# Expert weights of a mixture-of-experts stage as 2 MB tiles of 16 KB rows instead of 512 KB tiles of 4 KB rows

## The chip, the cores and the metric

The kernel runs on one core of one Trainium2 chip. The metric is the device time of one execution in microseconds; a version's time is the median of its runs. All data are float32. MB is a million bytes, but a tile called 512 KB or 2 MB holds 524,288 or 2,097,152 bytes.

## The reference, cut to what matters

The block has a mixing part (two gated branches over 512 rows of 1024 columns, called the front part here) and an expert part, which is what the change is about:

```
h = rmsnorm(x, g_ffn)                                  # 512 x 1024
aff = softmax(h @ w_router)                            # 16 experts
vals, idx = top_k(aff.T, 64)                           # every expert takes 64 rows
xe = h[idx]                                            # 16 x 64 x 1024
gt = einsum('ecd,edf->ecf', xe, w_gate)                # 16 x 64 x 2048
up = einsum('ecd,edf->ecf', xe, w_up)
ye = einsum('ecf,efd->ecd', silu(gt) * up, w_down) * vals
x  = x + scatter_add(ye, idx);  out = rmsnorm(x, g_final)
```

Each of the 16 experts has three matrices of 1024 x 2048 floats (w_down 2048 x 1024), 8.39 MB each: 48 matrices, 402.65 MB, each used once.

## The kernel before, in words

The front part projects with weights that are split in two fp32r halves. `w_raw` loads a raw column block into a `wr` tile (four buffers), `w_prep` splits it into `wh` (ScalarE) and `wl` (GpSimd), two buffers each, and `proj` multiplies. At the end `wo_load` and `wo_prep` do the same for `w_o` (its halves lie in `hT2`, a single tile that holds 16 slices), and a loop of 16 jobs (line 1076) multiplies by it and makes the router's logits (`turn`, `logits`).

Experts are served in pairs `pr` (expert 2pr in output rows 0 to 63, expert 2pr+1 in rows 64 to 127). A pair's 2048 hidden columns are done in two halves `c`. For each half `gate_part`, `up_part` and `down_part` go through eight weight tiles per expert; a tile is 128 x 1024 floats, 4 KB in one piece per partition. `unit_mm` holds the matmuls of gate and up. `gather` picks the pair's rows by matmuls with a one-hot matrix (line 1182) once per pair, `scatter` adds the pair's results to `xm` (line 1275). `down_part` of a half runs behind `gate_part` of the next.

All expert tiles are loaded by SyncE's queue at line 1010. The list `wq` has them in the order of use, and `WS` names for each the buffer it goes to: 38 buffers of 512 KB that are used in turn (`hA`, `we0`, `wh`, `wl`, `wr`, `we1`, `we2`), and seven more (`sg`, `st`, `ye`, `hh`) that serve once before their other use begins. Buffers belong to pools that open when the front part's pools close: `hA` and `we0` after the last projection, `we1` and the pool `T` (`sg`, `hh` and others) after the router's logits, `we2` after the top-64 search. `e_load(n)` issues the next n loads: 28, then 14, then 3, then 8 after every fourth weight tile of each expert. SyncE waits in order: a load whose buffer is still read holds up all loads behind it.

Of the kernel before, what the change touches and what calls it, by code (L numbers as in the profile page):

```python
# [25 lines left out]
EPS = 1e-6  # L26
KT = D // 128
# [3 lines left out]
for _n, _w in (("g_mix", 8), ("ca_w", 32), ("ca_b", 8), ("b_r", 16), ("b_i", 16), ("lam", 16),  # L31
               ("cb_w", 72), ("cb_b", 24), ("fbias", 16), ("g_ffn", 8)):
    CV[_n] = (_o, _w)
    _o += _w
# [7 lines left out]
    "W": ("right", dict(wr=4, wh=2, wl=2)),  # L42
# [10 lines left out]
    "hA": ("left", dict(hA=8)),  # L53
    "G": ("left", dict(tga=5)),
# [4 lines left out]
    "we0": ("left", dict(we0=12)),  # L59
    "T": ("right", dict(hh=4, xe=1, pm=1, sel=1, sg=1, st=1, ye=1)),  # L60
    "rout": ("right", dict(work=1, msk=1, aff=1, mx=1, sm=1, m8=1)),
    "we1": ("left", dict(we1=7)),
    "we2": ("left", dict(we2=3)),
# [34 lines left out]
def block_kernel(ctx, tc, A, out, dbg=None):  # L98
# [102 lines left out]
    for nm, c0 in (("w_in", 5120), ("w_a_out", 0)):  # L201
        wlist += [(nm, c0 + i * 128) for i in range(8)]
    wraw, wsp = {}, {}
# [759 lines left out]
    def wo_load(q):  # L963
        rs_ = []
        for j in range(2):
            r = t_([128, KT, 128], nm="wr")
# [15 lines left out]

    wq = []
    for v in range(17):
        order = [("w_gate", v), ("w_down", v - 1), ("w_up", v)]
        if v == 15:
            order[:2] = order[1::-1]
        for nm, n in order:
            if 0 <= n < 16:
                for u in range(8):  # L990
                    for e in (n // 2 * 2, n // 2 * 2 + 1):
                        wq.append((nm, e, n % 2, u))
    wq.insert(35, wq.pop(15))
    wtile = {}
    wn = [0]
    WS = ("hA",) * 8 + ("we0",) * 12 + ("wh", "wl") * 2 + ("wr",) * 4 + ("we1",) * 7 + ("we2",) * 3
    WS0 = WS[:35] + ("sg", "st", "ye") + ("hh",) * 4 + WS[35:]

    def e_load(n):
        for i in range(wn[0], min(wn[0] + n, len(wq))):  # L1000
            nm, e, c, u = wq[i]
            tag = WS0[i] if i < len(WS0) else WS[(i - len(WS0)) % len(WS)]
            t = t_([128, 1024], nm=tag)
# [7 lines left out]
            wtile[nm, e, c, u] = t  # L1011
            if i == len(wq) - 1:
                for hf in range(2):
                    for t_i, s_i in (last2, (t, src)):
                        h = slice(hf * 512, (hf + 1) * 512)
                        SY.dma_start(out=t_i[:, h], in_=s_i[:, h])
            last2 = t, src
        wn[0] = min(wn[0] + n, len(wq))

    def w_of(nm, e, c):  # L1020
        return [wtile.pop((nm, e, c, u)) for u in range(8)]

    for i in range(8):
# [3 lines left out]
        if i in (4, 5):  # L1027
            wo_load(i - 4)
# [3 lines left out]
    close_("G", "mB")  # L1032
    open_("pers", "we0", "xo")
    xm = t_([128, 4, D], nm="xm")
    for i in range(4):
# [11 lines left out]
    e_load(28 - wn[0])  # L1047
# [28 lines left out]
    for u, (q, i) in enumerate(jobs):  # L1076
# [12 lines left out]
        if i == 3 and q < 2:  # L1089
            wo_prep(q + 2)  # L1090
        if q == 2 and i == 3:
# [17 lines left out]
    e_load(14)  # L1109
# [43 lines left out]
    e_load(3)  # L1153
# [8 lines left out]

    def gather(pr, nb=2):

        pm = t_([128, 4, 128], nm="pm")
        for i in range(4):
            for e in range(2):
                o = pm[:, i, e * 64:(e + 1) * 64]
                pos = pT[:, i, 2 * pr + e:2 * pr + e + 1]
                if hh:  # L1170
# [3 lines left out]
        xe = t_([128, KT, 128], nm="xe")  # L1174
        yield xe
        n = KT // nb
        for b in range(nb):
            p = p2("m", 2)
            for k in range(n):
                c = (b * n + k) * 128  # L1180
# [3 lines left out]
            tt(V, xe[:, b * n:(b + 1) * n, :], p[:, 0:n * 128].rearrange("p (k c) -> p k c", k=n),  # L1184
               win(cv, [[1, n], [0, 128]], CV["g_ffn"][0] + b * n), ALU.mult)
# [22 lines left out]
    def unit_mm(out, xe, wa, wb, ks=range(KT)):  # L1208

        for k in ks:  # L1210
            for hf in range(2):
                for o, w in ((0, wa), (64, wb)):
                    T.matmul(out[hf][o:o + 64], lhsT=xe[:, k, o:o + 64], rhs=w[k][:, hf * 512:(hf + 1) * 512],  # L1213
                             start=(k == 0), stop=(k == KT - 1))
            if k in (3, 7):
                e_load(8)

    sg = []

    def gate_part(pr, c, xe):  # L1220
        ea, eb = 2 * pr, 2 * pr + 1
        pg = [p2("gu", 3), p2("gu", 3)]
        wa, wb = w_of("w_gate", ea, c), w_of("w_gate", eb, c)
        if pr == 0 and c == 0:
            next(first)
            for k in range(0, KT, 2):
                next(first)
                next(first, None)
                unit_mm(pg, xe, wa, wb, (k, k + 1))
        else:  # L1230
            unit_mm(pg, xe, wa, wb)
        if not sg:
            sg.extend((t_([128, 2, 512], nm="sg"), t_([128, 2, 4, 128], nm="st")))
        return pg

    def silu(pg):
        for hf in range(2):
            act(sg[0][:, hf, :], pg[hf], AF.Silu)

    def up_part(pr, c, xe):  # L1240
        ea, eb = 2 * pr, 2 * pr + 1
        pu = [p2("gu", 3), p2("gu", 3)]
        unit_mm(pu, xe, w_of("w_up", ea, c), w_of("w_up", eb, c))
        for hf in range(2):
            tt(V, sg[0][:, hf, :], sg[0][:, hf, :], pu[hf], ALU.mult)

    def down_part(pr, c, acc, between=lambda j: None):
        ea, eb = 2 * pr, 2 * pr + 1
        wa, wb = w_of("w_down", ea, c), w_of("w_down", eb, c)

        def turned(g):
            p = p2("tr", 1)
            for j in range(4):
                T.transpose(p[:, j * 128:(j + 1) * 128], sg[0][:, g, j * 128:(j + 1) * 128], ident)  # L1254
            act(sg[1][:, g].rearrange("p j c -> p (j c)"), p)
# [3 lines left out]
        for j in range(8):  # L1259
            for hf in range(2):  # L1260
                for o, w in ((0, wa), (64, wb)):
                    T.matmul(acc[hf][o:o + 64], lhsT=sg[1][:, j // 4, j % 4, o:o + 64],  # L1262
                             rhs=w[j][:, hf * 512:(hf + 1) * 512],
                             start=(c == 0 and j == 0), stop=(c == 1 and j == 7))
            if j == 0:
                turned(1)
            between(j + 1)
            if j in (3, 7):
                e_load(8)

    def scatter(ye, sc):
        for i in range(4):
            for hf in range(2):
# [4 lines left out]
                tt(V, v, v, p, ALU.add)  # L1278

    def ye_of(acc):  # L1280
        ye = t_([128, D], nm="ye")
        for hf in range(2):
            act(ye[:, hf * 512:(hf + 1) * 512], acc[hf])
        return ye
# [3 lines left out]
    last = []  # L1288

    def last_smat():  # L1290
        gfin = t_([128, D], nm="we0")
        SY.dma_start(out=gfin, in_=A["g_fin_b"])
# [4 lines left out]
        a = t_([128, D], nm="ye")[:, 0:S]  # L1297
# [5 lines left out]
        last.extend((oh, gfin))  # L1303

    hh = []

    def norms():

        for i in range(4):
            hh.append(t_([128, D], nm="hh"))  # L1310
            act(hh[i], xm[:, i, :], AF.Copy, scale=rs2[:, i:i + 1])
# [8 lines left out]
    later = {0: lambda: rows(1, 1, "gu", 3)}  # L1320
    first = gather(0, 8)
    xe = next(first)
    pend = None
    prev = None
    for pr in range(8):
        acc = [p2("acc", 2), p2("acc", 2)]
        for c in range(2):
            end = pr == 7 and c == 1
            if end:
                down_part(*prev)  # L1330
                prev = None
                last_smat()
            pg = gate_part(pr, c, xe)
            if pr == 0 and c == 1:
                norms()
            if prev is not None:
                down_part(*prev)
                if prev[1] == 1:
                    pend = (ye_of(prev[2]), smat(pr - 1))
            silu(pg)  # L1340
            if end:
                rows(0, 0, "m", 2)
                rows(0, 1, "m", 2)
                rows(1, 0, "gu", 3)
            if c == 1 and pr < 7:
                *_, nxe = gather(pr + 1)
            up_part(pr, c, xe)
            prev = (pr, c, acc)
            if c == 0 and pend:
                scatter(*pend)  # L1350
                pend = None
        xe = nxe

    preload(AF.Sqrt)
    oh, gfin = last
    down_part(*prev, lambda j: later.pop(j, lambda: None)())
    rows(2, 0, "gu", 3)
    yh = t_([128, D], F32R, nm="ye")
# [6 lines left out]
    hh = [t_([128, D], nm="hh") for _ in range(4)]  # L1365

# [154 lines left out]
```

## Time and profile before

| what | before |
|---|---|
| median of 3 runs (lowest to highest) | 1668.33 us (1667.86 to 1669.81) |
| the profiled execution: its own time / its span | 1668.91 us / 1667.1 us |
| TensorE (PE) busy | 1576.9 us, 95% of the span |
| VectorE / ScalarE / GpSimd busy | 593.4 / 370.3 / 375.1 us |
| packets of SyncE's and the other hardware queue q1 | 220272, 487.11 MB, 77.7% of 16 engines' span |

The span runs from the first to the last instruction; 1.8 us of the execution's own time lie around it. TensorE's busy time has modelled ends of matmuls in it, so 95% does not say that TensorE is what bounds the kernel: the chain of waits and the stretches by time do. The share of the DMA engines is the mean over 16 engines, and can exceed 100% because the packets of one engine overlap a little.

### The profile page before, as it was taken

How to read it: one execution, taken by the hardware profiler on the slowest of the kernel's cores; microseconds unless marked ns; L12 is line 12 of the kernel's file. 1: busy time of each engine (PE TensorE's matmuls, PEld its weight loads, DVE VectorE, ACT ScalarE, POOL GpSimd, SP SyncE). 2: the span in 40 equal slices, each digit the busy share in tenths (PEclk: the TensorE clock that was granted, in tenths of full speed). 3: DMA queues.
4: the chain of work that ended last, by engine and by line, in shares of the span. 5: the costliest groups of instructions: out<-in, count | busy, mean ns of one | idle time of the engine just before them, and what ended most of it. 6: DMA issues, size and time to landing. Idle time of an engine off the chain costs nothing.

```text
span 1667.1 us, 19022 instructions
## 1 busy us (share of the span) xinstructions
PE 1576.9 (95%) x7348; PEld 892.0 (54%) x7348; DVE 593.4 (36%) x872; ACT 370.3 (22%) x581; POOL 375.1 (23%) x256
## 2 busy tenths in 40 slices
PE   8999899999999999899999999999999999999996
PEld 5788788878888889534334343243242242242232
DVE  7887878786665663510010100200200200200103
ACT  5443322347565433201000000000000000000002
POOL 3646565557555741000000000000000000000000
PEclk9999999999999999999999999999999999999999
DMA  6566342543333329899999999999999999999996
GB/s 202 171 200 208 123 115 83 151 139 95 97 106 89 88 88 314 322 384 407 408 408 409 409 408 409 409 409 409 409 408 409 409 409 409 409 408 408 406 409 245
DMA packets 223046, 491.87 MB, mean 295 GB/s; under 512 B 17803, under 2 KB 112331, under 8 KB 222956
## 3 DMA queue, kind: packets, MB, share of 16 engines
q1 hardware_dynamic: 220272, 487.11, 77.7%
q10 hardware_dynamic: 2236, 1.98, 0.4%
q0 software_dynamic: 448, 1.57, 0.3%
q8 instruction: 58, 0.95, 0.2%
q14 instruction: 32, 0.26, 0.0%
HBM read 473.82 MB, written 16.78 MB: 294 GB/s over the span
## 4 chain that ended last, share of the span: by engine, by line
DMA 34%; PE 29%; DVE 2%; ACT 1%; issue 0%; SPq 0%; DVEq 0%; ACTq 0%
PE q L1213 11%; DMA we<-in_w_down_dram 7%; DMA we<-in_w_gate_dram 6%; DMA we<-in_w_up_dram 5%; PE q L1262 4%; PE q L1182 4%; PE ps L239 3%; PE ps L1084 3%; PE q L1275 3%; DMA hA<-in_w_up_dram 3%; DMA wr<-in_w_down_dram 2%; DMA hA<-in_w_down_dram 2%; DMA wh<-in_w_down_dram 2%; DMA hA<-in_w_gate_dram 2%; DMA wh<-in_w_up_dram 2%; DMA wr<-in_w_gate_dram 1%
## 5 line engine op out<-in xcount | busy, mean ns | idle before, releaser
L1213 PE MATMUL q<-we,xe 128*64 128x512 f32 x1160 | 322.5, 599 | 11.8 <-DMA we<-in_w_gate_dram 4.3
L128 POOL TENSOR_TENSOR hh<-hh,we 128x512 f32<-128x512 f32 x2 | 3.0, 1483 | 953.8 <-ACT hh L125 953.8
L128 POOL TENSOR_TENSOR wl<-wr,wh 128x1024 fp32r<-128x1024 f32 x72 | 181.1, 2519 | 145.1 <-ACT wh L125 66.1
L239 PE MATMUL ps<-hT,wh 128*128 128x512 f32 x880 | 210.4, 391 | 0.0
L1213 PEld LDWEIGHTS q<-we,xe 128*64 128x64 f32 x1160 | 97.0, 136 | 206.8 <-issue 138.5
L1262 PE MATMUL q<-we,st 128*64 128x512 f32 x600 | 177.5, 603 | 13.1 <-ACT st L125 6.7
L239 PEld LDWEIGHTS ps<-hT,wh 128*128 128x128 f32 x880 | 164.6, 188 | 35.3 <-issue 0.8
L125 ACT ACTIVATE st<-q 128x512 f32<-128x512 f32 x32 | 19.1, 597 | 701.8 <-PE q L1254 701.8
L128 DVE TENSOR_TENSOR xe<-q,cv 128x512 f32<-128x512 f32 (+1 forms) x22 | 11.4, 543 | 379.0 <-PE q L1213 362.7
L1213 PE MATMUL q<-hA,xe 128*64 128x512 f32 x472 | 136.5, 600 | 4.8 <-DMA hA<-in_w_up_dram 2.3
L239 PE MATMUL ps<-hT,wl 128*128 128x512 f32 x440 | 110.2, 393 | 0.6 <-POOL wl L128 0.6
L1262 PEld LDWEIGHTS q<-we,st 128*64 128x64 f32 x600 | 51.1, 136 | 108.7 <-issue 57.3
L131 DVE SCALAR_TENSOR_TENSOR pm<-q,slotc,pm 128x512 f32<-128x512 f32 x7 | 5.3, 751 | 255.7 <-ACT pm L125 255.7
L125 ACT ACTIVATE wh<-wr 128x1024 fp32r<-128x1024 f32 x72 | 76.2, 1058 | 90.4 <-PE ps L239 46.8
L239 PEld LDWEIGHTS ps<-hT,wl 128*128 128x128 f32 x440 | 83.6, 190 | 18.6 <-POOL wl L128 1.1
L1213 PEld LDWEIGHTS q<-hA,xe 128*64 128x64 f32 x472 | 41.3, 136 | 76.8 <-issue 50.7
L128 DVE TENSOR_TENSOR sg<-sg,q 128x512 f32<-128x512 f32 x32 | 21.3, 684 | 168.1 <-PE q L1213 168.1
L1213 PE MATMUL q<-wr,xe 128*64 128x512 f32 x188 | 65.3, 600 | 1.4 <-DMA wr<-in_w_up_dram 1.2
L239 PE MATMUL ps<-hA,wh 128*128 128x512 f32 x256 | 61.4, 392 | 0.0
L1262 PE MATMUL q<-hA,st 128*64 128x512 f32 x172 | 55.1, 603 | 3.4 <-ACT st L125 2.2
L1275 PE MATMUL q<-ye,pm 128*128 128x512 f32 x112 | 53.9, 619 | 0.0
L239 PEld LDWEIGHTS ps<-hA,wh 128*128 128x128 f32 x256 | 48.1, 188 | 10.5
(321 smaller groups left out, 2274.6 us busy)
## 6 DMA issues: line engine op xcount, KB each, us to landing
we<-in_w_down_dram SPq DMA_DIRECT2D x149, 512.0 KB, 10.2
we<-in_w_up_dram SPq DMA_DIRECT2D x147, 512.0 KB, 10.2
we<-in_w_gate_dram SPq DMA_DIRECT2D x143, 512.0 KB, 10.2
hA<-in_w_gate_dram SPq DMA_DIRECT2D x67, 512.0 KB, 10.2
wr<-in_w_in_dram SPq DMA_DIRECT2D x56, 512.0 KB, 4.3
hA<-in_w_up_dram SPq DMA_DIRECT2D x51, 512.0 KB, 10.2
hA<-in_w_down_dram SPq DMA_DIRECT2D x42, 512.0 KB, 10.2
wr<-in_w_down_dram SPq DMA_DIRECT2D x33, 512.0 KB, 10.2
```

Of the source, the lines that this page charges most:

```text
L125: P.activation(out=out, in_=in_, func=func, **kw)
L128: e.tensor_tensor(out=out, in0=a, in1=b, op=op)
L131: V.scalar_tensor_tensor(out=out, in0=a, scalar=s, in1=b, op0=op0, op1=op1)
L239: T.matmul(p, lhsT=a[:, k, :], rhs=b[k], start=(n == 0), stop=(n == 23))
L1084: T.matmul(p, lhsT=a[k][:, i * 128:(i + 1) * 128], rhs=wo[q][b][:, k, :], start=(n == 0), stop=(n == 23))
L1182: T.matmul(p[:, k * 128:(k + 1) * 128], lhsT=hh[i][:, c:c + 128] if hh else xm[:, i, c:c + 128], rhs=pm[:, i, :], start=(i == 0), stop=(i ...
L1213: T.matmul(out[hf][o:o + 64], lhsT=xe[:, k, o:o + 64], rhs=w[k][:, hf * 512:(hf + 1) * 512], start=(k == 0), stop=(k == KT - 1))
L1262: T.matmul(acc[hf][o:o + 64], lhsT=sg[1][:, j // 4, j % 4, o:o + 64], rhs=w[j][:, hf * 512:(hf + 1) * 512], start=(c == 0 and j == 0), sto ...
L1275: T.matmul(p, lhsT=sc[:, i * 128:(i + 1) * 128], rhs=ye[:, hf * 512:(hf + 1) * 512], start=True, stop=True)
```

## The change

An expert weight tile becomes 2 MB. For gate and up it is 256 rows of the full 2048 columns, two neighbouring rows per partition (row = 256u + 2p + r); for down it is 512 rows of 1024 columns, four neighbouring rows per partition. Either way 16 KB lie in one piece per partition in memory. `gather` takes every second column of its source (and a reordered `g_ffn`, `GX`), and the transposes of `down_part` every fourth, so that the operands fit these rows. A unit is now a whole pair: gate, up and down each go through four pairs of tiles over all 2048 columns, with four PSUM buffers for gate and up.

Buffers are slots of 16 KB per partition: two in `hz` (the place of `hA`), three in `we0`, one each in `whl`, `wring`, `we1`, `we2`, and one each in `sgy` and `hh` that serves once first. `wring` and `whl` are single tiles that take the place of the `wr`, `wh` and `wl` tiles. `e_load` issues as many loads as there are slots whose readers stand ahead in the program; it takes fresh slots first, then used ones in the order of their loads, and is called after every unit, that is after every two 2 MB tiles. The last pair of tiles is loaded in four pieces each. `scatter` is spread over the next unit's matmuls, and the rows of `xm` that the end adds are put into PSUM earlier. The second `wo_load` stands two slots later in the program than the first, not one.

```diff
-    "W": ("right", dict(wr=4, wh=2, wl=2)),
+    "W": ("right", dict(wring=1, whl=1)),
...
-    "T": ("right", dict(hh=4, xe=1, pm=1, sel=1, sg=1, st=1, ye=1)),
+    "T": ("right", dict(hh=1, xe=1, pm=2, sel=1, sgy=1)),
...
-        r = t_([128, KT, 128], nm="wr")
+        r = wring[:, i % 4]
         SY.dma_start(out=r, in_=A[src][:, c0:c0 + 128].rearrange("(k p) c -> p k c", p=128))
...
-        h = t_([128, KT, 128], F32R, nm="wh")
-        l = t_([128, KT, 128], F32R, nm="wl")
+        h, l = whl[:, i % 2, 0], whl[:, i % 2, 1]
...
+    def slots_of(t, n, first=False):
+        v = t if len(t.shape) == 2 else t.rearrange("p %s -> p (%s)" % (("a b c d e"[:2 * len(t.shape) - 3],) * 2))
+        for i in range(n // R):
+            wfresh.append((v[:, i * R * 2048:(i + 1) * R * 2048], first, [True]))
+    def e_load():
+        while wn[0] < len(wq):
+            q = wfresh or wslots
+            v, first, done = q[0]
+            i = wn[0]
+            if not done[0]:
+                break
+            q.pop(0)
+            wn[0] += 1
+            done = [False]
+            if not first:
+                wslots.append((v, False, done))
...
+            nm, e, u = wq[i]
             if nm == "w_down":
-                r0 = c * 1024 + u * 128
-                src = A[nm][e, r0:r0 + 128, :]
+                src = A[nm][e, u * 128 * RD:(u + 1) * 128 * RD, :].rearrange("(p s) c -> p (s c)", s=RD)
             else:
-                src = A[nm][e, u * 128:(u + 1) * 128, c * 1024:(c + 1) * 1024]
+                src = A[nm][e, u * 128 * R:(u + 1) * 128 * R, :].rearrange("(p r) c -> p (r c)", r=R)
+            wtile[nm, e, u] = v, done
             if i < len(wq) - 2:
-                SY.dma_start(out=t, in_=src)
+                SY.dma_start(out=v, in_=src)
+            elif i == len(wq) - 1:
+                w = R * 2048
+                cuts = [0] + ([w // 2] if R > 1 else []) + [w - 1024, w - 512, w]
+                for c0, c1 in zip(cuts, cuts[1:]):
+                    for v_i, s_i in (wlast[-1], (v, src)):
+                        SY.dma_start(out=v_i[:, c0:c1], in_=s_i[:, c0:c1])
...
+    slots_of(t_([128, 8 * 1024], nm="hz"), 4)
+    slots_of(we0, 6)
+    slots_of(t_([128, 4 * 1024], nm="whl"), 2)
...
-    e_load(28 - wn[0])
+    e_load()
...
         if i == 3 and q < 2:
             wo_prep(q + 2)
+            if q == 1:
+                slots_of(wring, 2)
+                e_load()
...
-    e_load(14)
+    slots_of(sgy, 2, True)
+    slots_of(hh, 2, True)
+    slots_of(we1, 2)
+    e_load()
...
-    e_load(3)
+    slots_of(we2, 2)
+    e_load()
...
-                    T.matmul(p[:, k * 128:(k + 1) * 128], lhsT=hh[i][:, c:c + 128] if hh else xm[:, i, c:c + 128], rhs=pm[:, i, :],
+                    T.matmul(p[:, k * 128:(k + 1) * 128], lhsT=src[:, i, u * 128 * R + r:(u + 1) * 128 * R:R], rhs=pm[:, i, :],
...
+    def rows_mm(out, xe, nm, pr, pace=lambda k: None):
+        for u in range(NU):
+            ws = [w_of(nm, 2 * pr + e, u) for e in range(2)]
+            for r in range(R):
+                k = u * R + r
+                for q in range(4):
+                    for o, (w, _) in zip((0, 64), ws):
+                        T.matmul(out[q][o:o + 64], lhsT=xe[:, k, o:o + 64], rhs=w[:, r * 2048 + q * 512:r * 2048 + (q + 1) * 512],
+                                 start=(k == 0), stop=(k == KT - 1))
+                pace(k)
+            for _, done in ws:
+                done[0] = True
+            e_load()
...
+        if pr == 0:
+            next(first)
+            rows_mm(pg, xe, "w_gate", pr, lambda k: k < 7 and next(first))
...
+            rows_mm(pg, xe, "w_gate", pr, lambda k: next(pend, None))
+            sc = smat(pr - 1)
+            acc = [p2("acc", 2), p2("acc", 2)]
+            down_part(pr - 1, acc, lambda g: g and silu(pg, g - 1))
+            silu(pg, 3)
+            ye_of(acc)
+            pend = scatter(sc)
+        if pr < 7:
+            *_, nxe = gather(pr + 1)
+        up_part(pr, xe)
...
-    for i in (0, 3, 1):
+    for i in (0, 3, 1, 2):
         add(i)
-    rows(2, 1, "tr", 1)
-    add(2)
```

## Rows read from the trace of the kernel before

**Rows 1.** The page: TensorE busy; 40 slices of DMA share and GB/s.

```profile
PE 1576.9 (95%) x7348; PEld 892.0 (54%) x7348; DVE 593.4 (36%) x872; ACT 370.3 (22%) x581; POOL 375.1 (23%) x256
...
DMA  6566342543333329899999999999999999999996
GB/s 202 171 200 208 123 115 83 151 139 95 97 106 89 88 88 314 322 384 407 408 408 409 409 408 409 409 409 409 409 408 409 409 409 409 409 408 408 406 409 245
```

**Rows 2.** The page: shares of the chain that ended last.

```profile
DMA 34%; PE 29%; DVE 2%; ACT 1%; issue 0%; SPq 0%; DVEq 0%; ACTq 0%
```

**Rows 3.** Chain that ended last, 750 to 1000 us: start, us, what.

```profile
772.04 7.34 PE q L1182 x64
779.38 13.93 PE q L1213 x64
...
877.42 7.34 PE q L1182 x64
...
917.10 10.16 DMA we<-in_w_down_dram
```

**Rows 4.** Stretches: length, engines' busy time, granted clock, DMA share, GB/s.

```profile
683.00:688.00 5.00, 4.36 (x36) 3.89 (x34) 1.59 (x10) 2.28 (x7) 0.15 (x1) 1.00 0.00 0
687.86:700.00 12.14, 6.05 (x12) 0.96 (x12) 10.46 (x28) 3.10 (x6) 0.00 (x0) 0.72 0.90 329
705.00:730.00 25.00, 24.94 (x138) 12.39 (x138) 3.76 (x14) 1.09 (x2) 1.34 (x2) 1.00 0.99 365
1000.00:1600.00 600.00, 569.80 (x2326) 199.87 (x2324) 59.94 (x122) 30.29 (x54) 0.00 (x0) 1.00 1.03 409
```

**Rows 5.** DMA queues and issues, 1000 to 1600 us: packets, MB, share of 16 engines.

```profile
DMA packets 67262, 245.19 MB, mean 409 GB/s; under 512 B 7472, under 2 KB 7472, under 8 KB 67235
...
q1 hardware_dynamic: 67235, 244.82, 102.3%
...
we<-in_w_gate_dram SPq DMA_DIRECT2D x91, 512.0 KB, 10.2
```

**Rows 6.** DMA queues, 500 to 600 us: packets, MB, share of 16 engines.

```profile
q1 hardware_dynamic: 17680, 8.91, 30.4%
```

**Rows 7.** Timeline of SyncE's queue, 560 to 760 us: start, us, loads issued.

```profile
640.59 6.39 SPq L1010 DMA_DIRECT2D hA<-in_w_gate_dram  x8
...
669.61 4.17 SPq L1010 DMA_DIRECT2D wr<-in_w_up_dram  x4
687.86 1.28 SPq L1010 DMA_DIRECT2D we<-in_w_up_dram  x3
```

**Rows 8.** Waits of SyncE's queue, 590 to 712 us: total, times, longest.

```profile
SPq L1010 <- PE ps L1068: 14.0, 1, 14.0
...
SPq L1010 <- DVE rt L1141: 3.7, 1, 3.7
```

**Rows 9.** Instructions on tile hT, 0 to 60 us: duration, first and last start.

```profile
L380 PE MATMUL ps<-hT,wh x16: 387/389/477, 16.2 to 20.9; 128*128 128x512 f32 x16
L125 ACT ACTIVATE hT<-ps,cv x8: 680/688/699, 13.3 to 17.9; 128x512 fp32r<-128x512 f32 x8
```

**Rows 10.** The page: the split of the projections' weights on GpSimd.

```profile
L128 POOL TENSOR_TENSOR wl<-wr,wh 128x1024 fp32r<-128x1024 f32 x72 | 181.1, 2519 | 145.1 <-ACT wh L125 66.1
```

**Rows 11.** Chain that ended last, 600 to 720 us: last product with w_o.

```profile
682.47 2.87 PE ps L1084 x24
```

**Rows 12.** Timeline, 704 to 730 us: first gather and the load behind the search.

```profile
704.40 0.84 SPq L1010 DMA_DIRECT2D we<-in_w_gate_dram  x2
...
705.84 3.17 PE L1182 MATMUL q<-pm,xm 128*128 128x128 f32 x24
707.33 0.29 DVE L128 TENSOR_TENSOR xe<-q,cv 128x128 f32<-128x128 f32 x1 [0.87 <-PE q L1182]
```

**Rows 13.** Chain that ended last, 1600 to 1668 us: rows of xm into PSUM.

```profile
1650.69 1.06 PE q L1318 x2
```

More of the change, by code (lines that the diff above doesn't have):

```diff
@@ L983, in block_kernel @@
     wq = []
-    for v in range(17):
+    for v in range(9):
         order = [("w_gate", v), ("w_down", v - 1), ("w_up", v)]
-        if v == 15:
+        if v == 7:
             order[:2] = order[1::-1]
         for nm, n in order:
[L989 to L994, printed above, removed]
-    wn = [0]
-    WS = ("hA",) * 8 + ("we0",) * 12 + ("wh", "wl") * 2 + ("wr",) * 4 + ("we1",) * 7 + ("we2",) * 3
@@ L1023, in block_kernel, with w_of @@
+            wlast.append((v, src))
+    def w_of(nm, e, u):
+        return wtile.pop((nm, e, u))
     for i in range(8):
@@ L1108, in block_kernel @@
     open_("T", "rout", "we1")
-    e_load(14)
+    sgy = t_([128, 4 * 1024], nm="sgy")
+    hh = t_([128, 4, D], nm="hh")
+    sg, ye = sgy[:, 0:2048], sgy[:, 2048:3072]
+    sts = [sgy[:, 3072 + i * 512:3584 + i * 512] for i in range(2)]
+    we1 = t_([128, 4 * 1024], nm="we1")
+    slots_of(sgy, 2, True)
+    slots_of(hh, 2, True)
+    slots_of(we1, 2)
+    e_load()
     aff = t_([128, 4, NE], nm="aff")
@@ L1206, in smat @@
         return s
[L1208 to L1234, printed above, removed]
@@ L1251, in turned, with silu, up_part, down_part @@
+    def silu(pg, g):
+        act(sg[:, g * 512:(g + 1) * 512], pg[g], AF.Silu)
+    def up_part(pr, xe):
+        pu = [p2("gu", 4) for _ in range(4)]
+        rows_mm(pu, xe, "w_up", pr)
+        for g in range(4):
+            c = slice(g * 512, (g + 1) * 512)
+            tt(V, sg[:, c], sg[:, c], pu[g], ALU.mult)
+    def down_part(pr, acc, turned_too=lambda g: None, between=lambda j: None):
         def turned(g):
-            p = p2("tr", 1)
+            p = p2("m", 2)
             for j in range(4):
-                T.transpose(p[:, j * 128:(j + 1) * 128], sg[0][:, g, j * 128:(j + 1) * 128], ident)
@@ L1255, in turned @@
-            act(sg[1][:, g].rearrange("p j c -> p (j c)"), p)
+                u, i = divmod(4 * g + j, RD)
+                T.transpose(p[:, j * 128:(j + 1) * 128], sg[:, u * 128 * RD + i:(u + 1) * 128 * RD:RD], ident)
+            act(sts[g % 2], p)
+            turned_too(g)
         turned(0)
         between(0)
[L1259 to L1269, printed above, removed]
@@ L1271, in scatter @@
-    def scatter(ye, sc):
+        for u in range(NU):
+            ws = [w_of("w_down", 2 * pr + e, u) for e in range(2)]
+            for i in range(RD):
+                j = u * RD + i
+                st = sts[j // 4 % 2]
+                for hf in range(2):
+                    for o, (w, _) in zip((0, 64), ws):
+                        T.matmul(acc[hf][o:o + 64], lhsT=st[:, j % 4 * 128 + o:j % 4 * 128 + o + 64],
+                                 rhs=w[:, i * 1024 + hf * 512:i * 1024 + (hf + 1) * 512],
+                                 start=(j == 0), stop=(j == 15))
+                if j % 4 == 0 and j < 12:
+                    turned(j // 4 + 1)
+                between(j + 1)
+            for _, done in ws:
+                done[0] = True
+            e_load()
@@ L1352, in block_kernel @@
         xe = nxe
     preload(AF.Sqrt)
[L1355 to L1358, printed above, removed]
+    later = {1: (0, 0, "gu", 4), 2: (0, 1, "gu", 4), 3: (1, 0, "gu", 4), 4: (1, 1, "gu", 4), 10: (2, 0, "m", 2),
+             11: (2, 1, "m", 2)}
+    acc = [p2("acc", 2), p2("acc", 2)]
+    down_part(7, acc, between=lambda j: j in later and rows(*later[j]))
+    gfin = wtile[None]
+    yh = t_([128, 4 * 1024], F32R, nm="sgy")[:, 0:D]
@@ L1442, in block_kernel @@
     store(P, 2, 1)
-    close_("we2", "we1", "we0", "pers", "hA", "base", "T", "W")
+    close_("we2", "we1", "we0", "pers", "hz", "base", "T", "W")
 def _tables():
```

146 lines of the change are left out of this document (60 added, 86 removed).

## The prediction, made before the changed kernel ran

> **What bounds the kernel now.** I read the page first. TensorE shows 95% busy, but the DMA engines run at 9 tenths and 408 to 409 GB/s in every slice from the 19th to the last but one [rows 1], and the chain that ended last is 34% DMA and 29% TensorE [rows 2]; two resources are near their ends, and the order in time has to say which one. The chain by time does: until 917 us it runs from matmul to matmul, one pair taking 877.42 - 772.04 = 105.4 us, and from 917 us on it steps from landing to landing, 10.2 us each [rows 3]. So TensorE is behind at first, catches up at 917 us, and from there the expert loads set the end. A landing of 10.2 us for 512 KB is not a slow transfer: 409 GB/s pass a tile in 1.28 us, and 8 x 1.28 = 10.2, so eight loads are in flight and the queue is never empty. The stretches show this from 1000 to 1600 us (409 GB/s) and where the queue did run empty: 0 GB/s from 683 to 688, slow to start after 687.86, and 365 GB/s from 705 to 730 [rows 4].
>
> The end is therefore: when the stream starts, plus bytes over rate, plus the stretches in which it is dry, plus what follows the last landing. I go through these four.
>
> **Rate of the stream.** Two stretches with packets of different size give what a packet costs. From 1000 to 1600 us the queue moved 67,235 packets, 244.82 MB, in 102.3% of 16 x 600 us = 9,821 us of engine time; 7,472 of the packets are the small ones that report a load as done, one for each engine and tile, the others are 4 KB [rows 5]. From 500 to 600 us, where the rows of a tile are 512 B, 17,680 packets with 8.91 MB took 30.4% of 1,600 us = 486.4 us [rows 6]. With a cost a for each packet and b for each byte: 67,235a + 244.82e6 b = 9,821e3 ns and 17,680a + 8.91e6 b = 486.4e3 ns, so b = 0.0378 ns and a = 8.5 ns. A 512 KB tile is, on one engine, 8 packets of 4 KB and one report: 9a + 32,768b = 1,314 ns; four of them 5,258 ns. A 2 MB tile in pieces of 16 KB is 9a + 131,072b = 5,029 ns, 4.35% less, so 409 becomes 427.6 GB/s. No load of this trace has a piece over 4 KB, so this is the law carried beyond its rows. Its bounds: if 16 KB travel as four packets, only three of four reports go: 33a + 131,072b = 5,233 ns, 0.5% less; the most that could go is every fixed cost, 4,953 ns, 5.8%. I take 4.35%, because the fit is made of the same queue's packets and 16 KB is the piece that the diff asks for. Bytes that the rate acts on: 402.65 MB of weights and 0.52 MB of g_fin, less the 28 tiles (14.68 MB) before the dry stretch at 683 us, which is 388.5 MB; at 409 GB/s 949.9 us. The gain is 0.0435 x 949.9 = 41.3 us (bounds 4.7 and 55).
>
> The fixed cost that I read from the rows, 8.5 ns, is where the Trainium skill speaks against the change: "DMA: Bandwidth & Descriptors", section "Why small descriptors are slow (HBM only)", gives about 3 cycles per packet and 32 bytes of description per operation, and holds that joining pieces pays only up to 256 B. With the 850 MHz and 32 B a cycle of its section "Where 436 GB/s comes from" that is 4 cycles, 4.7 ns, an estimate from that page; 24 fewer packets would save 113 of 5,258 ns, 2.1%, 20 us in place of 41. The rows do not agree with so small a cost, but they reach only to 4 KB.
>
> **Start of the stream.** Loads are issued from 640.59 us, behind the loads of `xm` and `w_o`, which stay; the 28th tile is issued by 673.45 (669.61 plus four loads of 1.28) and the next at 687.86 [rows 7], after a wait of 14.0 us for the last router logits [rows 8]. Seven new slots (`hz` 2, `we0` 3, `whl`, `wring`) hold the same 14 MB, so a faster rate there only lengthens the dry stretch: nothing. The first load after it now goes to `sgy`, in the pool `T` over `hT2` and `mh`, whose last reader ends at 682.47 + 2.87 = 685.3 us [rows 11], not over the logits' tiles: 2.5 us earlier, if the addresses fall as I lay the pools out; nothing if not. I take 2.5.
>
> **Front part.** `wring` and `whl` put slices of one tile where tiles of their own were. This costs nothing as long as waits go by slices: `hT` is such a tile, and its first matmul starts at 16.2 us while ScalarE still starts a write to its last slice at 17.9 [rows 9]. Without that cover a split could not overlap the projection before it, and at least the 2.5 us of the GpSimd part would stand on the chain in each of 72 splits, 181 us [rows 10]. The second `wo_load` is issued later in the program, but its buffers wait for splits that don't move.
>
> **Dry stretches.** From an issue into an empty queue to full flow the trace loses 12.14 x (1 - 329/409) = 2.4 us [rows 4]. With 2 MB slots that come free in pairs the arithmetic is this. `sgy`, `hh` and `we1` (6.29 MB) flow from 687.8 to 702.5. The slot `we2` lies over tiles of the top-64 search; before, the load that did so waited 3.7 us for it [rows 8] and left at 704.40 [rows 12]; flow 706.8, so 4.3 us dry. Its 2.1 MB end at 711.7. Then nothing is free until TensorE has used unit 0. The first gathered slice is ready at 707.33 + 0.29 = 707.6 [rows 12]; 64 matmul records of a half pass over eight k take 13.93 us [rows 3], so one k over all columns takes 13.93 x 2/8 = 3.5 us and a unit of two 7.0. Between each two k there is now one gather block (3.17/3 = 1.1 us) and the wait for its VectorE copy (about 0.5 with its hand-over), so the first k costs 3.5 us and each further one 1.1 + 0.5 + 3.5 = 5.1: unit 0 ends at 716.2, and with 2.4 and a hand-over flow is back at 718.7: 7.0 us dry. A unit then takes 10.2 us, just over the 9.8 that 4.19 MB take, and the slots of the four units keep the stream busy until 757.9. The last unit ends at 746.8; TensorE runs the next gather, 7.3 us, and an up unit, 7.0, before it frees a slot again: flow 763.7, 5.8 us dry. From then on a unit frees 4.19 MB every 7.0 us against 9.8, and a lead builds that the later gathers and scatters no longer use up. Sum 17.1 us; the old kernel lost 25 x (1 - 365/409) = 2.7 in the same place [rows 4]. Cost: 14.4 us. Its bounds: nothing, if the stream is as smooth as before, and about 25, if the weight loads of TensorE from every second column go at half speed (no row shows a strided one): the gather is bound by its weight loads, so 7.3 us more in the first gather between units and 1 more in each block.
>
> **What TensorE does later** costs nothing while it waits for data: a pair takes it 105.4 us, and 24 tiles take the stream 50.33/0.4276 = 117.7. The same matmuls are made; transposes, `silu` and `norms` are only moved, under those 12 us. If the cover went, each us of a pair would cost 8.
>
> **The tail.** The chain has two matmuls on rows of `xm`, 1.06 us, behind the last down product [rows 13]; they move ahead, but the copies of the result run beside them, so I take 0.5 us. The last tiles are cut to the same 256 KB pieces as before.
>
> Sum against the profiled execution (span 1667.1, 1.8 us around it, 1668.9): -41.3 - 2.5 + 14.4 - 0.5 = -29.9, so 1639.0. The median of the runs is 0.6 lower: 1638.
>
> **Rivals.** First, the fixed cost is about half of what I fitted, because in the stretch of 512 B rows every burst starts on idle engines and its packets carry that start. Then 24 x 4.2 of 5,258 ns go, 1.9%, 18.3 us; the dry stretches come to 15.6, and the time is 1668.3 - 18.3 - 2.5 + 12.9 - 0.5 = 1660. The share of 30.4% speaks for it, the same queue against. The skill's page above lies near this case. Second, and on the other side: 16 KB pieces travel as packets of 4 KB, so the change of rows does nothing and the coarse slots remain: -4.7 - 2.5 + 12.0 - 0.5 = +4.3, 1673, slower. For it speaks that no packet of a load exceeds 4 KB here, but no piece does either. It decides where the rate gains less than about 1%. Third, TensorE's pair exceeds the stream's 117.7 us, as when strided weight loads and waits add over 12.3 us to 105.4; then no lead builds and the 5.8 us of dryness return in each of seven more pairs: 1638 + 41 = 1679. Doubled weight loads alone would add 7.3 for the gather and some 2.4 for sixteen transposes, which stays below.
>
> **How the numbers follow.** Forecast 0.68; half the fixed cost 0.10; packets of 4 KB 0.14; TensorE the bound 0.08. A difference of 0.2%, 3.3 us, is about what a measurement can tell from none. Faster: the first two, and the best end of the others, 0.80; same 0.05, the second rival's better end; slower 0.15. The likeliest case's own range is 1625 (dry stretches nearly as short as before) to 1649 (25 us more of them). The range reaches to 1673, to take in the first rival and the middle of the second: 1625 to 1673.
>
> **What would show it.** Right: 425 to 429 GB/s in the stretch from 1000 to 1600 us, a packet count near a quarter, dry stretches near 704, 715 and 760 us, a chain that steps from landing to landing in the second half. Wrong: still 409 to 411 GB/s, or packets as many as before; SyncE waiting for matmuls beyond 800 us; a first expert load issued later than at 640.59 us.

## The result and the profile after

The changed kernel takes 1652.41 us (median; 1651.99 to 1653.23) against 1669.07 us of the kernel before on the same chip: a ratio of 0.9899, with a 95% interval of 0.9885 to 0.9912. The prediction had said 1638 us (1625 to 1673), so the time lies inside its range, 14 us above its value and 3 us above the 1625 to 1649 of its likeliest case. The profiled execution took 1652.69 us, 16.2 less than that of before. One run of all, of the kernel with both cuts below, took 5631 us at a granted clock of 0.345 and is set apart from the comparisons.

The page of the changed kernel, the rows that answer to [rows 1, 2]:

```profile
PE 1552.5 (94%) x7348; PEld 894.5 (54%) x7348; DVE 592.2 (36%) x870; ACT 371.9 (23%) x581; POOL 376.8 (23%) x258
...
DMA  6556433443333337877999999999999999999994
GB/s 203 167 187 209 147 94 105 144 135 98 102 102 90 90 91 264 351 282 310 429 427 428 426 428 427 428 429 427 427 428 428 427 427 429 427 427 428 427 428 194
...
PE 49%; DMA 12%; DVE 3%; ACT 1%; issue 1%; DVEq 0%; ACTq 0%
```

From the 20th slice to the last but one the stream runs at 426 to 429 GB/s instead of 406 to 409. But the 18th and 19th slices fall to 282 and 310, where before they were at 384 and 407, and the chain that ended last now consists of TensorE for one half of the span and of landings for 12% only.

The stream from 1000 to 1600 us, as [rows 5]:

```profile
DMA packets 17608, 256.50 MB, mean 427 GB/s; under 512 B 1951, under 2 KB 1951, under 8 KB 1951
...
q1 hardware_dynamic: 17585, 256.16, 100.4%
...
we<-in_w_down_dram SPq DMA_DIRECT2D x27, 2048.0 KB, 31.3
```

17,585 packets in place of 67,235, for more bytes: the 16 KB pieces travel whole.

Stretches of the changed kernel, as [rows 4] (length, busy time and instructions of TensorE, its weight loads, VectorE, ScalarE and GpSimd, granted clock, DMA share, GB/s):

```profile
686.05:700.00 13.95, 7.44 (x25) 2.46 (x25) 10.85 (x33) 5.05 (x11) 0.00 (x0) 0.65 0.95 375
700.00:720.00 20.00, 17.75 (x75) 6.78 (x76) 7.69 (x21) 0.00 (x0) 2.42 (x4) 0.99 0.52 177
720.00:750.00 30.00, 28.08 (x145) 12.47 (x142) 2.80 (x11) 2.39 (x4) 0.00 (x0) 1.00 0.97 392
750.00:780.00 30.00, 30.00 (x165) 14.21 (x166) 0.00 (x0) 4.59 (x4) 0.00 (x0) 1.00 0.72 268
780.00:1600.00 820.00, 773.83 (x3368) 289.17 (x3366) 84.89 (x176) 46.65 (x82) 0.00 (x0) 0.97 1.01 427
```

Each stretch loses its length times one less its rate over 427 GB/s: 1.7, 11.7, 2.5 and 11.2 us, 27 in all before 780 us, and nothing behind. To make the account exact, here are the bytes of the queue that carries the loads (packets, MB, share of 16 engines) in the kernel before, from 686 to 780 and from 780 to 1600 us:

```profile
q1 hardware_dynamic: 9744, 35.52, 97.6%
...
q1 hardware_dynamic: 91879, 334.56, 102.3%
```

and the same two stretches of the changed kernel:

```profile
q1 hardware_dynamic: 1947, 28.49, 78.8%
...
q1 hardware_dynamic: 24035, 350.04, 100.4%
```

At 780 us the changed kernel is 7.0 MB behind; by 1600 us it is 8.4 MB ahead. From the 820 us the rates are 408.0 and 426.9 GB/s, so the 388.5 MB behind the router take 910.1 us in place of 952.2: 42.2 us won. The loss before 780 us is 93.95 - 28.49/0.4269 = 27.2 us after and 92.14 - 35.52/0.408 = 5.1 us before: 22.1 us given back. The first load behind the router goes at 686.05 us, 1.8 sooner than in [rows 7]. With 388.5 - 378.5 = 10.0 MB left at 1600 us the flow would be over at 1623.4 us, and with 18.4 MB at 1645.2 before: 21.8 us sooner. The spans end 27.5 and 21.9 us behind that, which is 5.6 us lost after the stream. Sum: -42.2 - 1.8 + 22.1 + 5.6 = -16.3.

SyncE's queue in that stretch, as [rows 7] (start, us, loads issued):

```profile
642.39 2.16 SPq L1030 DMA_DIRECT2D hz<-in_w_gate_dram  x2
...
686.05 0.33 SPq L1030 DMA_DIRECT2D sgy<-in_w_gate_dram  x1
686.43 0.43 SPq L1030 DMA_DIRECT2D hh<-in_w_up_dram  x1
688.54 16.69 SPq L1030 DMA_DIRECT2D we<-in_w_up_dram  x2
717.67 0.80 SPq L1030 DMA_DIRECT2D hz<-in_w_up_dram  x2
728.02 10.69 SPq L1030 DMA_DIRECT2D we<-in_w_up_dram  x3
738.80 0.38 SPq L1030 DMA_DIRECT2D whl<-in_w_gate_dram  x1
748.73 0.33 SPq L1030 DMA_DIRECT2D wring<-in_w_gate_dram  x1
763.53 7.15 SPq L1030 DMA_DIRECT2D we<-in_w_gate_dram  x2
770.77 6.78 SPq L1030 DMA_DIRECT2D hz<-in_w_gate_dram  x2
```

Units 0, 1 and 2 of the first gate product each give back two slots: the row at 717.67, two of the three loads of the row at 728.02, and its third, 10 us on, with the load at 738.80. Unit 3 gives back one, at 748.73, and so does the first unit of up, at 763.53 (the row's second load follows 7 us later, a unit on): their partners lay in `sgy` and `hh`, which serve once.

The end of the chain (start, us, what), as [rows 13]:

```profile
1566.40 30.05 DMA we<-in_w_down_dram
...
1596.50 1.93 PE q L1290 x6
...
1624.83 8.79 PE q L1290 x40
```

From the landing at 1596.45 to 1633.62 us TensorE never waits again: the last down product runs 37.1 us in one piece, while the stream runs dry at about 1623. Before, the chain stepped from landing to landing until 1646.9, and 3.73 us of matmuls followed.

### The profile page after: what moved, and what is told of

It is laid out like the page before. It is cut to its first block, busy times and chain, and to the rows that moved or that the text cites. A ratio compares the mean times of both kernels' runs of the same rounds, so it can differ in the third digit from the quotient of the medians.

```text
span 1650.9 us, 17905 instructions
## 1 busy us (share of the span) xinstructions
PE 1552.5 (94%) x7348; PEld 894.5 (54%) x7348; DVE 592.2 (36%) x870; ACT 371.9 (23%) x581; POOL 376.8 (23%) x258
## 4 chain that ended last, share of the span: by engine, by line
PE 49%; DMA 12%; DVE 3%; ACT 1%; issue 1%; DVEq 0%; ACTq 0%
PE q L1255 21%; PE q L1290 14%; DMA we<-in_w_up_dram 8%; PE q L1305 4%; PE ps L245 3%; PE ps L1107 3%; DMA hz<-in_w_up_dram 2%; DMA we<-in_w_down_dram 2%; PE q L1221 2%; PE q L1277 1%; PE q L1240 0%; PE q L1342 0%; DVE work L1167 0%; DVE m L1164 0%; PE ps L1091 0%
## 5 line engine op out<-in xcount | busy, mean ns | idle before, releaser
L245 PE MATMUL ps<-hT,whl 128*128 128x512 f32 x1320 | 309.0, 393 | 1.0 <-POOL whl L133 0.6
L245 PEld LDWEIGHTS ps<-hT,whl 128*128 128x128 f32 x1320 | 249.0, 189 | 55.3 <-POOL whl L133 1.1
L133 POOL TENSOR_TENSOR whl<-wring,whl 128x1024 fp32r<-128x1024 f32 x72 | 182.0, 2531 | 145.5 <-ACT whl L130 66.5
L1290 PE MATMUL q<-we,sgy 128*64 128x512 f32 x576 | 191.2, 622 | 3.9 <-ACT sgy L130 3.6
L1255 PE MATMUL q<-hz,xe 128*64 128x512 f32 x480 | 161.9, 604 | 4.5 <-DMA hz<-in_w_up_dram 3.7
L1255 PE MATMUL q<-wring,xe 128*64 128x512 f32 x240 | 107.9, 596 | 0.8 <-DVE xe L133 0.8
L1255 PE MATMUL q<-whl,xe 128*64 128x512 f32 x208 | 93.6, 596 | 4.4 <-issue 4.1
L130 ACT ACTIVATE whl<-wring 128x1024 fp32r<-128x1024 f32 x72 | 76.2, 1058 | 91.1 <-PE ps L245 49.1
L245 PE MATMUL ps<-hA,whl 128*128 128x512 f32 x384 | 90.9, 395 | 0.0
L1290 PE MATMUL q<-hz,sgy 128*64 128x512 f32 x224 | 75.7, 614 | 1.5 <-ACT sgy L130 1.5
## 6 DMA issues: line engine op xcount, KB each, us to landing
we<-in_w_up_dram SPq DMA_DIRECT2D x35, 2048.0 KB, 29.9
hz<-in_w_gate_dram SPq DMA_DIRECT2D x14, 2048.0 KB, 27.5
```

The source lines that it names most:

```text
L130: P.activation(out=out, in_=in_, func=func, **kw)
L133: e.tensor_tensor(out=out, in0=a, in1=b, op=op)
L245: T.matmul(p, lhsT=a[:, k, :], rhs=b[k], start=(n == 0), stop=(n == 23))
L1255: T.matmul(out[q][o:o + 64], lhsT=xe[:, k, o:o + 64], rhs=w[:, r * 2048 + q * 512:r * 2048 + (q + 1) * 512], start=(k == 0), stop=(k == KT ...
L1290: T.matmul(acc[hf][o:o + 64], lhsT=st[:, j % 4 * 128 + o:j % 4 * 128 + o + 64], rhs=w[:, i * 1024 + hf * 512:i * 1024 + (hf + 1) * 512], s ...
```

## The experiments

Each was timed beside the kernel before on the same chip (medians of 1669 to 1670 us); a ratio is to that. Three questions: is the rate the matter of packets, what makes the stream dry, and what makes the end late.

**Pieces of 4 KB in the changed kernel.** Same slots, units and order; each load goes as four:

```diff
-                SY.dma_start(out=v, in_=src)
+                for c in range(0, R * 2048, 1024):
+                    SY.dma_start(out=v[:, c:c + 1024], in_=src[:, c:c + 1024])
```

> The changed kernel with each 2 MB load issued as four loads of 512 KB, each with 4 KB in one piece per partition; slots, units and their order as in the changed kernel. If the fixed cost of a packet sets the rate, the stream falls back to 409 to 411 GB/s from 1000 to 1550 us and its end moves some 41 us later; TensorE then waits more and is less far behind at the end, so the time is about 1680 us (1674 to 1690). If larger slots or more bytes in flight made the rate, it stays at 427 GB/s and the time at 1652 us.

Measured: 1684.18 us, ratio 1.0085 (1.0066 to 1.0104). From 1000 to 1550 us:

```profile
q1 hardware_dynamic: 61689, 224.64, 102.4%
```

224.64 MB in 550 us are 408.4 GB/s, the rate of before. The pieces are the whole of the gain in rate, and the slots and units without them make the kernel 15 us slower.

**Pieces of 8 KB in the changed kernel.** The same with two loads of 2048 columns.

> The slots, units and order of the changed kernel; only each 2 MB load is issued as two loads of 1 MB with 8 KB in one piece per partition. Packet theory: on one engine 16 packets and two reports, 18 x 8.5 + 131,072 x 0.0378 = 5,108 ns for 2 MB instead of 5,029, so 421 GB/s in place of 427 in the waiting stage and about 1661 us, a third of the way from the changed kernel to the one with 4 KB pieces (1684). Rival, that what counts is pieces over 4 KB or not: 427 GB/s and 1652 us. Rival, that only 16 KB pieces are fast: 409 and 1684.

Measured: 1661.46 us, ratio 0.9952 (0.9936 to 0.9968); from 1000 to 1550 us:

```profile
q1 hardware_dynamic: 31738, 231.12, 101.1%
```

231.12 MB in 550 us, 420.2 GB/s: the packet law's value, not one of the rivals'. Three sizes now lie on one line: 2 MB take one engine 5.13, 4.99 and 4.91 us of the stretch at 36, 18 and 9 packets (reports counted), which is 8.0 and 8.8 ns for each packet less. Packets and loads go together in these runs, nine packets for each load on each engine, so they alone can't tell a cost of each packet from one of each load. [rows 6] speak for the packet: at 79 ns for a load on each engine (9 x 8.8) the 17 loads there would take 22 us and their bytes 337, some 358 of the 486 us measured; that the rest comes from starts on idle engines, the first rival's reason, no run excludes.

**Without the scatter.** TensorE's additions of pairs 0 to 6 to `xm` are left out (the list `pend` stays empty), so the output lacks those pairs' results.

> The changed kernel without the scatter of pairs 0 to 6: 112 matmul records of TensorE and 56 additions of VectorE are left out, 8.5 us of TensorE for a pair, so the output lacks those pairs' results; the loads are unchanged. If TensorE, which in the changed kernel runs without a break from 1597 to 1634 us while the stream ends at about 1622, is what is late at the end, the last down product moves to within 3 us of the end of the stream and the time falls by about 10 us to 1642 (1639 to 1645), the stream's end staying within 3 us. If the end follows the stream, with the landing's own delay, it stays at 1652 us.

Measured: 1653.33 us, ratio 0.9901 (0.9878 to 0.9924): the time of the changed kernel. TensorE was busy for 724.8 us from 780 to 1600 us, where the changed kernel had 773.8, and its last product began no sooner:

```profile
1564.59 32.59 DMA we<-in_w_down_dram
...
1597.22 1.93 PE q L1290 x6
...
1625.55 8.78 PE q L1290 x40
```

So 49 us of TensorE's work lie under the stream for nothing, and the theory that it comes late by the sum of its work falls. What starts the last product is the landing of its first unit.

**Rows of xm out of the last product.** The six pairs of matmuls that put rows of `xm` into PSUM leave the last down product; VectorE adds these rows to the sums afterwards.

```diff
-    down_part(7, acc, between=lambda j: j in later and rows(*later[j]))
+    down_part(7, acc)
...
+    add_x(0, 0)
+    add_x(0, 1)
     squares(0)
```

> The changed kernel with the 12 matmul records (6.4 us) that put rows of xm into PSUM taken out of the last down product; VectorE adds xm behind the last sums instead (six more additions of 0.69 us). If TensorE is late at the end, the last down product ends 5 to 6 us earlier, of which VectorE's additions take 1 to 3 back: about 1648.5 us (1646 to 1651). If the stream sets the end, the down product ends when it did and the additions cost 1 to 4 us: 1654 (1653 to 1657).

Measured: 1653.90 us, ratio 0.9905 (0.9887 to 0.9924), no gain. The 6.4 us are gone from TensorE, and a landing stands in their place:

```profile
1585.77 32.90 DMA we<-in_w_down_dram
1618.67 0.04 issue
1618.71 1.93 PE q L1290 x6
1620.64 0.68 PE q L1277 x4
1621.32 12.22 PE q L1290 x56
```

With less to do TensorE waits for the whole third unit, and after it 14.8 us of two units are left, to 1633.5: the same end as with the rows, in an execution in which the load to `sgy` went 1.9 us later (687.97 and 686.05). At most some 2 us are won there, and behind the product VectorE's additions take about 3 us more in this execution (20.5 us to the end of the span in place of 17.3). So TensorE's work and the landings end close together.

**The second gather behind the first up product.** TensorE then comes to the first up units sooner, and the first gather is begun two blocks ahead.

```diff
             next(first)
-            rows_mm(pg, xe, "w_gate", pr, lambda k: k < 7 and next(first))
+            next(first)
+            rows_mm(pg, xe, "w_gate", pr, lambda k: k < 6 and next(first))
...
-        if pr < 7:
+        if 0 < pr < 7:
             *_, nxe = gather(pr + 1)
         up_part(pr, xe)
         if pr == 0:
+            *_, nxe = gather(1)
             norms()
```

> The changed kernel with the second pair's gather moved behind the first pair's up product, and the first gather kept two blocks ahead of its user. The first slot after the first gate product then comes free some 8 us earlier (755.7 in place of 763.5 us). If the dry stretches at the start shift the whole stream, the one near 760 us nearly goes and the time falls by about 7 us to 1645.5 (1643 to 1648). If TensorE's own work sets the end from the start to the end, nothing changes: 1652 us.

Measured: 1642.86 us, ratio 0.9838 (0.9819 to 0.9858). Its stretches:

```profile
700.00:720.00 20.00, 19.00 (x90) 8.15 (x90) 6.99 (x20) 0.00 (x0) 2.43 (x4) 1.00 0.49 170
...
750.00:780.00 30.00, 28.66 (x160) 14.10 (x157) 4.78 (x11) 1.15 (x1) 0.00 (x0) 1.00 1.00 417
```

The third dry stretch is gone (417 GB/s in place of 268: 30 x 149/427 = 10.5 us), the first is untouched (170 and 177). From 720 to 750 us it is 419 for 392 GB/s, which gives back 1.9 us more of flow. The order alone gives back 9.5 us of time, so most of a dry stretch shows at the end.

**Tiles of 1 MB, with and without the new order.** `R = 1` in place of `R = 2`: 8 KB pieces, slots and units of half the size.

> Tiles of 1 MB with 8 KB pieces (half the rows per tile) in the changed kernel: twice as many slots of half the size, units of half the length. Packet theory: 421 GB/s, which costs 388.5 MB x (1/0.421 - 1/0.427), some 13 us against the changed kernel. Slot theory (the dry stretches and the late end come from slots that return 2 MB at a time and units of 7 us): the dry stretches fall to about half of their 25 us and the last product starts about 3 us sooner, so 13 us come back and the time is about 1652 (1648 to 1657). If the slots' size doesn't matter: 1665. If the rate doesn't change either way: 1639.

> Tiles of 1 MB with 8 KB pieces, and the second gather put behind the first up product, the first one begun two blocks ahead. By the slot theory most of the dry stretches is then gone by two ways at once, so less is left to win than the 9.5 us that the order alone brought with 2 MB tiles: rate +13, tail -3, dry stretches -15 to -18 against the changed kernel: 1645 (1641 to 1649). If 2 MB and the order are as good in the dry stretches and only the rate differs: 1656 (1642.9 + 13).

Measured: 1661.21 us, ratio 0.9950 (0.9935 to 0.9965), and with the order 1646.91, ratio 0.9864 (0.9847 to 0.9880). The first is 9 us above what I expected of the slot theory. Its stretches say why:

```profile
700.00:720.00 20.00, 17.45 (x67) 5.60 (x66) 9.61 (x25) 0.00 (x0) 2.42 (x4) 0.97 0.74 292
...
750.00:780.00 30.00, 30.00 (x172) 14.73 (x170) 0.00 (x0) 5.42 (x6) 0.00 (x0) 1.00 0.60 244
```

Smaller slots halve the first stretch's loss, 20 x (1 - 292/421) = 6.1 us for 11.7, but not the third's: 30 x (1 - 244/421) = 12.6. In this execution the load to `sgy` went 2.8 us later (688.83); counted from that load instead of by the clock the two are 6.4 and 12.5 us, so the reading stands, and the later start is 2.8 of the 9 us. The third stretch isn't made by the size of a slot but by what stands between the last gate unit and the first up unit. With both edits it came out near what was expected, 2 MB and the order being better by 4 us.

**Smaller pieces where TensorE waits at the end.** The kernel with the new order, and the last pair's loads of up and down cut into two pieces of 8 KB, the two tiles of a unit by turns:

```diff
-                SY.dma_start(out=v, in_=src)
+                if nm != "w_gate" and e >= 14:
+                    for c in (0, 2048) if e % 2 else ():
+                        for v_i, s_i in (wlast[-1], (v, src)):
+                            SY.dma_start(out=v_i[:, c:c + 2048], in_=s_i[:, c:c + 2048])
+                else:
+                    SY.dma_start(out=v, in_=src)
```

> The kernel with the order of the gathers changed (1642.9 us), and the last pair's loads of up and down cut into two pieces of 8 KB, the two tiles of a unit by turns, so that TensorE can start on the first half of a unit before its end has landed. Theory that TensorE is late at the end because a unit lands whole: the last product starts and ends 2 to 3.5 us sooner, 1640. Theory that the stream alone sets the end: 33.6 MB go at 421 in place of 427 GB/s, +1 us, 1644.

Measured: 1639.49 us, ratio 0.9818 (0.9804 to 0.9833), 3.4 us under the order alone, with intervals that overlap. Before the cut, the chain waits for a whole unit of up and runs 30 matmuls behind it:

```profile
1545.80 29.96 DMA hz<-in_w_up_dram
...
1575.80 8.78 PE q L1255 x30
```

and with the cut it waits for half a unit:

```profile
1559.80 19.80 DMA hz<-in_w_up_dram
...
1579.65 3.65 PE q L1260 x14
```

The landing in this row is 3.8 us later, but what follows it is 5.1 us shorter, and the last product begins at 1584.7 in place of 1585.9, in an execution in which SyncE's load to `sgy` had gone 4.1 us later (689.08 and 685.03).

**Smaller pieces where SyncE waits at the start.** The first pair's loads of up and down cut likewise, so that a slot can be filled by halves, alone and together with the cut at the end:

```diff
+                elif nm != "w_gate" and e < 2:
+                    for c in (0, 2048):
+                        SY.dma_start(out=v[:, c:c + 2048], in_=src[:, c:c + 2048])
```

> The kernel with the other order of the gathers and the last pair's loads cut (1639.5 us), and the up and down loads of the first pair cut into two pieces of 8 KB as well, so that a slot of unit 0 can be refilled by halves. Slot theory: in the dry stretch between 700 and 720 us a first half goes out some 3.5 us (half a unit) sooner, and so for each later wait for a slot until the lead is built: 1636 (1634 to 1638). Rival, that SyncE's order holds the halves up anyway (the second half of one tile stands ahead of the first half of the next): no change, 1639.5.

> The same cut of the first pair's loads alone, without the cut of the last pair's. Slot theory: 3 us less than the 1642.9 of the kernel with only the order changed, 1640; and some 3 us over the kernel with both cuts, since the late end is then there again. Rival, SyncE's order: 1643.

Measured: 1639.13 us, ratio 0.9819 (0.9805 to 0.9832), and 1642.34 us, ratio 0.9837 (0.9823 to 0.9850). The cut at the end is worth 3.2 us once more, here timed side by side; the cut at the start nothing. The reason that I had given the rival (SyncE's order) is not what happened: in the kernel with both cuts the first half did go out sooner, 26.9 us after the load to `sgy` where it was 31.6 in the kernel with the new order alone.

```profile
686.82 0.33 SPq L1038 DMA_DIRECT2D sgy<-in_w_gate_dram  x1
...
713.67 6.00 SPq L1036 DMA_DIRECT2D hz<-in_w_up_dram  x4
```

What it won in the first dry stretch it lost behind:

```profile
700.00:720.00 20.00, 19.02 (x84) 7.77 (x84) 8.71 (x23) 0.00 (x0) 2.42 (x4) 0.96 0.67 239
720.00:750.00 30.00, 30.00 (x152) 11.97 (x150) 1.17 (x4) 4.66 (x6) 0.00 (x0) 1.00 0.99 405
750.00:780.00 30.00, 28.67 (x153) 12.91 (x150) 4.78 (x11) 2.33 (x3) 0.00 (x0) 1.00 0.97 386
```

By the clock that is 239 for 170 GB/s, then 405 for 419 and 386 for 417, but a part is only the load to `sgy`, which went 1.8 us later here (from 686 to 700 us 344 for 403). Counted from that load, the stretch from 14 to 34 us behind it has 233 in place of 178 GB/s, 1.1 MB more, and the one from 64 to 94 us 385 in place of 418, 1.0 MB less; the flow lost in the first 124 us is 15.6 us here and 15.7 there. The reason, as I read it and did not try: until a lead is built, the bytes that the stream can have moved are the slots that TensorE has freed, and its pace was the same.

The kernel with the cut at the end and the one with both cuts, at 1639 us, are the fastest versions: 13 us below the changed kernel.

## Why the prediction was right in kind and 14 us too low

The gain came from where it was forecast. That the time lies in the range is in part luck: the likeliest case's own range ended at 1649, below the time, and only the width that was added for rivals which did not happen takes it in.

**Rate: right.** 426.9 GB/s for the 427.6 forecast, a gain of 42.2 us for 41.3. The fit on 512 B and 4 KB rows carried to 16 KB: it gave 8.5 ns for a packet, and the three sizes on the chip give 8.0 and 8.8. This also settles the first two rivals: packets of 4 KB did not happen, and half the fixed cost would have left the rate at 417. From the Trainium skill's "DMA: Bandwidth & Descriptors", section "Why small descriptors are slow (HBM only)", I had worked out an estimate of 4.7 ns and 20 us; the runs show a larger cost, 8.0 to 8.8 ns and 42 us. The Trainium skill's 256 B, in the same section, are said of joining consecutive descriptors into a packet; here the pieces themselves grow, so I was wrong to hold that sentence against the change.

**Start of the stream: right within what one profile can tell.** 1.8 us sooner for 2.5. The front part itself isn't that steady: over eleven profiles of kernels in which it is the same, the load to `sgy` goes between 685.0 and 692.6 us, so neither this term nor the 1.8 us by which the first expert load went later (642.39 for 640.59) is shown to be the change's.

**Dry stretches: the step that was mis-sized.** 17.1 us were forecast and 24.8 came (27.2 less the 2.4 of the first start); against before 22.1 for 14.4. The first two stretches were right: 4.3 and 7.0 forecast near 704 and 715, 11.7 measured from 700 to 720. From 720 to 750 us 2.5 more went, which the sum had put at nothing: it had a unit of 10.2 us against 9.8 us of stream, and the rows from 717.67 to 748.73 show 10.3 to 10.4, some half a microsecond for each unit. The third was the main error: "the slots of the four units keep the stream busy until 757.9" counted eight slots, but one of the eight, `sgy`, serves once, and of the first up unit's two slots one is `hh`. SyncE's rows show one load at each of these places where I had two. A load is 4.9 us of stream, so the first of them alone makes 10.7 us of the 5.8; from 750 to 780 us 11.2 went. That these two slots are the cause is read from the rows and not tried alone; that most of the stretch shows at the end, and that the wait of the first up product makes it, is shown by the new order (-9.5 us). The upper bound, weight loads from every second column at half speed, did not come: a pair's gather takes 7.74 us in place of 7.34, its weight loads 196 ns in place of 192.

**TensorE later: right.** A pair stays under the stream's time: 49 us less of its work changed nothing. The third rival is out: behind 780 us the stream loses nothing. But two of the signs that I had named came out otherwise. SyncE does wait for matmuls beyond 800 us (800 to 1600 us: total, times, longest),

```profile
SPq L1030 <- PE q L1255: 440.7, 64, 13.9
SPq L1030 <- PE q L1290: 239.1, 30, 14.8
```

and the chain does not step from landing to landing; it has one landing for each pair:

```profile
1080.68 32.94 DMA we<-in_w_up_dram
...
1199.33 32.80 DMA hz<-in_w_up_dram
```

From one to the next are 118.7 us, of which the chain puts 86 on TensorE; the 24 tiles of a pair take the stream 50.33/0.4269 = 117.9 us. A load is issued when a matmul frees its slot and lands some 30 us later, so about six are in flight (30 x 0.4269/2.097), and waits of SyncE of up to 14.8 us leave the stream at 427 GB/s. Neither sign therefore shows that TensorE is the bound.

**The tail: the second step that failed.** -0.5 us was forecast and +5.6 came. I looked only at the last pair of tiles, which is cut as before. All units ahead of it land whole, two tiles of 2 MB at once, and a unit is then 7 us of TensorE. The last product of four units, with its transposes and rows of `xm`, is 37.1 us of TensorE behind the landing of its first unit; the other three units take the stream only 12.6 MB / 0.4269 = 29.5 us. With 512 KB tiles TensorE followed the landings to the last. The cut of the last pair's loads gave 3.2 us of it back. Taking away the rows alone did not, since the same whole landing stood behind them. Of the 5.6 us, 0.9 lie behind the last down product (17.3 us to the end of the span in place of 16.4): the 0.5 that the two matmuls moved ahead were to save does not show. The other runs fit: by the same account of bytes and rate the span ends 27.5 to 29.3 us behind the flow in the five versions whose last units of up land as whole 2 MB tiles, and 22.8 to 25.7 in the six with smaller pieces or tiles there; before, 21.9. How smaller pieces shorten it is shown for the cut alone: with pieces of 4 KB the last product, too, runs in one piece, for 37.7 us.

Sum of the misses: +7.7 (dry) + 6.1 (tail) + 0.7 (start) - 0.9 (rate) = 13.6 us, the difference between -29.9 and -16.3.

## What to carry to other kernels

Where a stream of loads sets the time, find the cost of a packet from two stretches with different packets and multiply it by the packets that go: here 27 fewer on each engine for 2 MB were worth 42 us in 950. Then pay for the coarser tiles separately: count slot by slot what TensorE frees and when, leaving out buffers that serve once, and put work that frees no slot behind work that does. At the end of the stream, cut not only the last tile but every load that the last two products wait for, since what is left to do when a tile lands grows with the tile.

## What the hardware showed beside that

TensorE's granted clock falls in the waiting stage, where before it stood at 1.00 [rows 4]: 0.97 from 780 to 1600 us in the changed kernel, whose landings come two tiles at a time. From 1000 to 1600 us TensorE waited at most 0.2 us for a landing before, and up to 2.7 us here. In the kernel with the new order, the stretches around the last wait for a unit of up:

```profile
1568.00:1575.76 7.76, 5.10 (x24) 1.44 (x20) 0.00 (x0) 0.00 (x0) 0.00 (x0) 1.00 0.99 422
1575.76:1580.00 4.24, 4.20 (x14) 1.37 (x16) 0.00 (x0) 0.00 (x0) 0.00 (x0) 0.64 1.02 433
1580.00:1584.60 4.60, 4.60 (x21) 1.32 (x17) 2.06 (x3) 0.00 (x0) 0.00 (x0) 0.96 1.03 438
```

After 2.7 us without work TensorE starts again at a mean of 0.64 of 2.4 GHz, which means at the 1.2 GHz level for the greater part of 4.2 us, and the 30 matmuls take 8.78 us. Not every such wait does that: in the kernel without the rows of `xm` TensorE waited 2.65 us at the same place, and the 28 matmuls behind it took 6.25 us at the full clock; in the changed kernel four of the five waits of 2.7 us between 780 and 1600 us were followed by a mean of 0.60 to 0.62 over 4.2 us, and one by 1.00. In the middle of the stream this costs nothing, since TensorE waits there anyway; on the last wait it is some 2 us of the end. With the cut, whose waits are 1.3 us, the same place ran at 1.00. A part of the cut's 3.2 us may then be the clock's; how much was not measured by itself.
